# Grouped-query attention on one core: every matmul as a 64-row tile of the array, q, k and v cast by DMA, q and k also transposed by it, and the order of work fixed in the program

## The chip, the cores and the metric

The kernel runs on one core of a Trainium2 chip. Its time is device time in microseconds (us), the median of several runs. The profile is one execution, and its span is about 1.8 us shorter than the time of the same run. In this text PE or TensorE is the matmul engine, ACT or ScalarE computes the exponentials, DVE or VectorE the normalization, POOL or GpSimd issues DMAs that cast, and SP or SyncE issues the others.

## The reference

```python
batch, n_q_heads, n_kv_heads, seq, head_dim = (8, 8, 2, 1024, 64)   # q, k, v in f32, times 0.1
# four query heads share a key/value head
scores = scale * np.matmul(q_group, k_group.transpose(0, 1, 3, 2))  # scale = 1/8
attn = np.exp(scores - scores_max)
attn = attn / (np.sum(attn, axis=-1, keepdims=True) + 1e-08)
output = np.matmul(attn, v_group)
```

Both kernels leave out the maximum, which is harmless with inputs this small, and get the denominator from a column of ones beside v. A **cell** is 128 keys by 512 queries of one head; there are 8 x 8 x 2 x 8 = 1024. Three cells share one exponential instruction.

## The kernel before

It loads q, k and v as f32, transposes q and k on TensorE, and lets a scheduler order everything by priority. One side of a head pair is selected by a k that is padded with zeros to 128 rows.

```python
    def transpose_group(stages, lo, name_pool):          # 64 of these
        tp = tpool.tile([128, NSC, 128], BF16, name="tpsum")
        for sc in range(NSC):
            nc.tensor.transpose(tp[:, sc, :], _hi16(stages[sc])[:, lo : lo + 2, :], ident)
        dst = name_pool.tile([128, NSC, 128], BF16, name="xT")
        nc.vector.tensor_copy(out=dst, in_=tp)
    ...
    def score_wave(gw, qT, kT):
        sps = spool.tile([128, CPERW, QBS], FP32, name="spsum")       # two buffers
        with tc.high_priority(offset=1 << 20):                        # scores go first
            for slot, gc in enumerate(cells):                         # three cells
                nc.tensor.matmul(sps[:, slot, :], lhsT=kT[b][g][side][:, c, :],   # 128 rows
                                 rhs=qT[(b, pair)][...], start=True, stop=True)
        nc.scalar.activation(out=pt[:, 0:n, :], in_=sps[:, 0:n, :], func=AF.Exp, scale=scale)
    ...
    def output_block(b, pair, side, qb, pts, vt):        # 128 of these, 32 matmuls each
        ops = opool.tile([128, NQS, D + 1], FP32, name="opsum")       # one buffer
        for qs in range(NQS):
            for c in range(NKC):
                nc.tensor.matmul(ops[:, qs, :], lhsT=..., rhs=_hi16(vt[b][g][:, c, :]),
                                 start=(c == 0), stop=(c == NKC - 1))
        nc.vector.reciprocal(out=rec, in_=ops[:, :, D])
        nc.vector.tensor_tensor(out=ost, in0=ops[:, :, 0:D], in1=rec..., op=ALU.mult)
```

The softmax here doesn't subtract the row's maximum and nothing guards it: scores larger than these inputs give would overflow.

## Time and profile before

| | before |
|---|---|
| time, median of 4 runs measured beside the changed kernel | 479.99 us (479.82 to 480.41) |
| exponentials | 342, ends 1.343 us apart |
| start of the first exponential | 13.8 us |
| time lost between exponentials | 3.2 us |
| from the end of the last exponential to the end | 4.5 us |

The last three rows are read from the trace. I take the end of every exponential, subtract it from the next end, and call what exceeds 1.343 us lost. The sum must close: 13.8 + 3.2 + 4.5 = 21.5, and 480.1 - 21.5 = 458.6 us is the exponentials' own work.

The profiled execution, with its span of 480.1 us, was some 2 us slower than the median run.

### The profile page before, as it was taken

Reading aid. Unit: us, or ns where it says so; the run is one execution under the profiler, and the core shown is the slowest. Engines: PE = TensorE matmul, PEld = TensorE weight load, DVE = VectorE, ACT = ScalarE, POOL = GpSimd, SP = SyncE. Lnnn points to the kernel's source line nnn. Section 1 sums busy time; section 2 is a strip of 40 time slices with the busy share of each in tenths; the row PEclk is TensorE's granted clock in tenths of the full one; section 3 lists DMA queues with packets and bytes.
Section 4 is the critical chain, followed back from the end, with each engine's and each line's share of the span. In section 5 each row is a group of like instructions: output and inputs, shape, how many; then the busy total and the mean of one; then the engine's idle time right before and its main releaser. Section 6 shows DMA issues by size and latency. Waiting matters only on the chain.

```text
span 480.1 us, 13304 instructions
## 1 busy us (share of the span) xinstructions
PE 443.3 (92%) x5632; PEld 282.6 (59%) x5632; DVE 129.3 (27%) x400; ACT 460.2 (96%) x343; POOL 141.1 (29%) x198
## 2 busy tenths in 40 slices
PE   2999999999999999999999999999999998988895
PEld 1566666666666666666565656656565555555553
DVE  3332233232242323222241312313222111111112
ACT  1699999999999999999999999999999999999996
POOL 9993056128047111830138010111100111101011
PEclk9999999999999999999999999999999999999999
DMA  7997356138157122842148121211212111111111
GB/s 177 218 227 182 79 142 169 45 90 219 35 125 198 47 55 58 197 109 58 35 115 206 34 56 46 67 34 35 56 45 58 40 39 35 46 34 34 46 34 45
DMA packets 109883, 42.82 MB, mean 89 GB/s; under 512 B 105728, under 2 KB 105728, under 8 KB 109824
## 3 DMA queue, kind: packets, MB, share of 16 engines
q1 hardware_dynamic: 102656, 25.18, 24.8%
q0 software_dynamic: 7168, 16.79, 11.1%
q8 instruction: 44, 0.72, 0.6%
q14 instruction: 15, 0.12, 0.1%
HBM read 25.17 MB, written 16.78 MB: 87 GB/s over the span
## 4 chain that ended last, share of the span: by engine, by line
ACT 72%; PE 21%; issue 3%; POOL 1%; DMA 1%; DVE 1%; POOLq 0%
ACT pt L191 72%; PE spsum L183 13%; PE opsum L204 6%; PE tpsum L107 2%; POOL qstage L87 1%; DMA qstage<-in_q_dram 1%; DVE ost L216 0%; DVE xT L111 0%; DVE rec L214 0%; POOL ident masks.py:199 0%; POOL ident masks.py:197 0%; POOLq masks.py:199 0%; POOLq L277 0%
## 5 line engine op out<-in xcount | busy, mean ns | idle before, releaser
L191 ACT ACTIVATE pt<-spsum 128x1536 bf16<-128x1536 f32 x342 | 458.9, 1706 | 14.6 <-PE spsum L183 14.6
L183 PE MATMUL spsum<-xT 128*128 128x512 bf16 x1024 | 278.2, 380 | 23.5 <-ACT pt L191 19.0
L204 PEld LDWEIGHTS <-pt 128*128 128x128 bf16 x4096 | 174.0, 98 | 75.9 <-DVE ost L216 16.9
L204 PE MATMUL opsum<-vstage,pt 128*128 128x65 bf16 x4096 | 191.1, 195 | 1.1 <-DVE ost L216 1.0
L183 PEld LDWEIGHTS <-xT 128*128 128x128 bf16 x1024 | 98.5, 97 | 94.2 <-issue 35.8
L222 POOL DMA_DIRECT2D out_dram<-ost x64 | 48.3, 755 | 316.1 <-DVE ost L216 283.6
L214 DVE RECIPROCAL rec<-opsum 128x4 f32<-128x4 f32 x128 | 23.4, 183 | 309.2 <-PE opsum L204 300.4
L87 POOL DMA_DIRECT2D qstage<-in_q_dram x128 | 92.2, 723 | 18.4 <-PE tpsum L107 12.8
L216 DVE TENSOR_TENSOR ost<-opsum,rec 128x256 f32<-128x256 f32 x128 | 53.8, 421 | 3.7 <-DVE rec L214 0.2
L111 DVE COPY xT<-tpsum 128x1024 bf16<-128x1024 bf16 x64 | 43.6, 681 | 32.9 <-PE tpsum L107 20.7
L107 PE MATMUL tpsum<-ident,kstage 128*128 128x128 bf16 x256 | 28.5, 226 | 5.4 <-DMA kstage<-in_k_dram 5.3
L107 PE MATMUL tpsum<-ident,qstage 128*128 128x128 bf16 x256 | 27.4, 225 | 3.3 <-DVE xT L111 1.6
L107 PEld LDWEIGHTS <-kstage 128*128 128x128 bf16 x256 | 18.9, 101 | 14.0 <-issue 5.7
L107 PEld LDWEIGHTS <-qstage 128*128 128x128 bf16 x256 | 18.6, 101 | 9.8 <-issue 2.8
L77 DVE MEMSET kstage<- 128x192 f32 x64 | 13.5, 218 | 2.3 <-PE tpsum L107 0.9
L191 ACT ACT_TABLE_LOAD x1 | 1.3, 1283 | 0.7 <-PEq L277 0.7
L96 DVE MEMSET vstage<- 128x8 f32 x16 | 0.9, 65 | 0.0
masks.py:199 POOL TENSOR_SCALAR_AFFINE_SELECT ident<-ident 128x128 bf16<-128x128 bf16 x1 | 0.3, 307 | 0.1
masks.py:197 POOL MEMSET ident<- 128x128 bf16 x1 | 0.2, 205 | 0.3 <-POOLq L277 0.3
L277 POOL MEMSET const-float32-0.0<- 128x1 f32 x1 | 0.1, 99 | 0.2 <-issue 0.2
L277 POOL MEMSET const-bfloat16-1.0<- 128x1 bf16 x1 | 0.1, 102 | 0.0
L277 POOL MEMSET const-uint8-127<- 128x1 uint8 x1 | 0.1, 102 | 0.0
(1 smaller groups left out, 0.1 us busy)
## 6 DMA issues: line engine op xcount, KB each, us to landing
qstage<-in_q_dram POOLq DMA_DIRECT2D x128, 64.0 KB, 3.7
qstage<-in_q_dram SPq DMA_DIRECT2D x128, 64.0 KB, 3.4
out_dram<-ost SPq DMA_DIRECT2D x64, 128.0 KB, 1.9
out_dram<-ost POOLq DMA_DIRECT2D x64, 128.0 KB, 2.3
kstage<-in_k_dram SPq DMA_DIRECT2D x64, 64.0 KB, 2.7
vstage<-in_v_dram SPq DMA_DIRECT2D x16, 256.0 KB, 3.1
```

Of the source, the lines that this page charges most:

```text
L77: nc.vector.memset(ks[:, 0::2, :], 0.0)
L87: eng.dma_start(out=qstage[sc][:, 2 * j : 2 * j + 2, :], in_=q[b, 2 * j : 2 * j + 2].rearrange("h (sc p) d -> sc p h d", p=128)[sc],)
L96: nc.vector.memset(vs[:, :, D], 1.0)
L107: nc.tensor.transpose(tp[:, sc, :], _hi16(stages[sc])[:, lo : lo + 2, :], ident)
L111: nc.vector.tensor_copy(out=dst, in_=tp)
L183: nc.tensor.matmul(sps[:, slot, :], lhsT=kT[b][g][side][:, c, :], rhs=qT[(b, pair)][:, qb * NQS : (qb + 1) * NQS, :], start=True, stop=True,)
L191: nc.scalar.activation(out=pt[:, 0:n, :], in_=sps[:, 0:n, :], func=AF.Exp, scale=scale)
L204: nc.tensor.matmul(ops[:, qs, :], lhsT=pts[gc // CPERW][:, gc % CPERW, qs * 128 : (qs + 1) * 128], rhs=_hi16(vt[b][g][:, c, :]), start=(c ...
L214: nc.vector.reciprocal(out=rec, in_=ops[:, :, D])
L216: nc.vector.tensor_tensor(out=ost, in0=ops[:, :, 0:D], in1=rec.unsqueeze(2).to_broadcast([128, NQS, D]), op=ALU.mult,)
L222: (nc.gpsimd if (qb + side) % 2 else nc.sync).dma_start(out=out[b, h].rearrange("(qs p) d -> p qs d", p=128)[:, qb * NQS : (qb + 1) * NQS, :],
L277: nc = _bacc.Bacc("TRN2", target_bir_lowering=False, num_devices=1)
```

## The change

Its intent is to take work from TensorE. Two 64-row matmuls on the two halves of the array are meant to run side by side. The transposes leave TensorE for the DMA engines. The scheduler is switched off: the program's order is the order of every engine. The core of the diff, with cuts:

```diff
-            eng.dma_start(out=qstage[sc][...], in_=q[b, 2 * j : 2 * j + 2]...)   # f32, 64 KB each
-            nc.tensor.transpose(tp[:, sc, :], ..., ident)
-        nc.vector.tensor_copy(out=dst, in_=tp)
+        nc.gpsimd.dma_start(out=kscr..., in_=k[b]...)          # casts f32 to bf16, into DRAM
+        nc.sync.dma_start_transpose(out=kt, in_=kscr)
+        for j in range(NPAIR):                                 # four of q: five transposes in a row
+            nc.gpsimd.dma_start(out=qscr..., in_=q[b, j::NPAIR]...)
+            nc.sync.dma_start_transpose(out=qt, in_=qscr)
 ...
-                    lhsT=kT[b][g][side][:, c, :],
+                lhsT=kT[b][side * D : (side + 1) * D, c * 128 : (c + 1) * 128],
 ...
+        for c in (2 * part, 2 * part + 1):
+            for qs in range(NQS):
+                for rows in range(2):
+                    side = rows ^ half                         # the halves swap heads mid-unit
+                    lo = rows * 64
+                    mm = nc.tensor.matmul(
+                        ops[:, side, qs * (D + 1) : (qs + 1) * (D + 1)],
+                        lhsT=pcell[(u * NKC + c, side)][lo : lo + 64, qs * 128 : (qs + 1) * 128],
+                        rhs=vt[(b, side)][lo : lo + 64, c, :], ...)
+                    if half == 1 and c == 0 and qs == 0:
+                        tc.add_manual_dep(mm.ins, turn[0].name, SYNC, reason="bank")
+        if step == NKC // 2 - 1:
+            turn[0] = nc.sync.nop().ins                        # the turn
+            tc.add_manual_dep(turn[0], last.ins.name, SYNC, reason="bank")
 ...
+    with tc.manual_schedule():
+        load_batch(0)
+        for i in range(NSTEP + LAG):                           # 512 steps, LAG = 10
+                if i % per_batch == 4 and i // per_batch + 1 < B:
+                    load_batch(i // per_batch + 1)
+                score_step(i)                                  # two score matmuls
+                output_step(i - LAG)                           # sixteen output halves
```

A **unit** is now two heads by 512 queries, 16 cells, 8 steps; there are 64. A **step** is two scores and sixteen output halves. The **turn** is the moment in the middle of a unit when the halves of the array swap accumulators; TensorE then waits for a no-op on SyncE.

## The prediction

> **What bounds the kernel now.** I read the page first (busy times, then the chain that ended last), then the waits, then the groups, and last the timeline of a few microseconds in the middle.
>
> ```profile
> span 480.1 us, 13304 instructions
> ...
> PE 443.3 (92%) x5632; PEld 282.6 (59%) x5632; DVE 129.3 (27%) x400; ACT 460.2 (96%) x343; POOL 141.1 (29%) x198
> ...
> ACT 72%; PE 21%; issue 3%; POOL 1%; DMA 1%; DVE 1%; POOLq 0%
> ...
> L191 ACT ACTIVATE pt<-spsum 128x1536 bf16<-128x1536 f32 x342 | 458.9, 1706 | 14.6 <-PE spsum L183 14.6
> L183 PE MATMUL spsum<-xT 128*128 128x512 bf16 x1024 | 278.2, 380 | 23.5 <-ACT pt L191 19.0
> L204 PE MATMUL opsum<-vstage,pt 128*128 128x65 bf16 x4096 | 191.1, 195 | 1.1 <-DVE ost L216 1.0
> ```
>
> Two engines look full, but only one of them sets the time. ScalarE is idle 14.6 us before exponentials, in three places, and the list of waits shows that most of that is one gap, the start:
>
> ```profile
> ACT pt L191 <- PE spsum L183: 14.6, 3, 11.8
> PEld L204 <- DVE ost L216: 16.9, 60, 0.9
> ```
>
> Outside those three places an exponential follows the one before without a gap. Three of them take 4.41 us from the first start to the last end in the timeline below, and the median one lasts 1.727 us (the view of that line), so they start (4.41 - 1.727) / 2 = 1.343 us apart. 342 x 1.343 = 459.3 us. The first starts at 13.82 and the end comes about 4.5 us after the last: 13.8 + 459.3 + 4.5 = 477.6, plus some 2.5 us of early gaps. **The kernel is its exponentials.**
>
> ```profile
> 200.67 4.41 ACT L191 ACTIVATE pt<-spsum 128x1536 bf16<-128x1536 f32 x3
> 202.01 0.46 PE L204 MATMUL opsum<-vstage,pt 128*128 128x65 bf16 x9
> ...
> 202.44 0.81 PE L183 MATMUL spsum<-xT 128*128 128x512 bf16 x3
> ```
>
> TensorE's 92% is not its work. A score matmul is counted 380 ns, but three in a row take 0.81 us, so they start (0.81 - 0.38) / 2 = 0.215 us apart. Nine output matmuls take 0.46 us, (0.46 - 0.195) / 8 = 33 ns apart, weight load included. Work per exponential: 3 x 0.215 + 12 x 0.033 = 1.04 us of 1.343. TensorE has 0.3 us to spare per exponential, and the scheduler puts the three score matmuls of a tile together, directly after the wait for ScalarE. So a faster TensorE by itself can give nothing here: the most that remains to be won is at the start and the end.
>
> **What the Trainium skill says.** "ScalarE: Activation LUTs", section "What ACT_TABLE_LOAD costs", gives an ACTIVATE with immediate scale 186 ns + 0.833 ns per element, of which 93 ns overlap back to back: 1.37 us for 1536. The trace has 1.343, so it agrees and the engine is at its rate. "TensorEngine Tiling (Array Packing)", "Key Properties", says that different tiles can load weights and multiply in parallel; no run here shows it yet. "TensorE: Matmul & The Clock Gate", "LDWEIGHTS", says that a load costs by its columns, not its rows: a 64-row load of 128 columns would be no cheaper than a 128-row one, and the change doubles their number. "DMA: Bandwidth & Descriptors", "SWDGE vs HWDGE vs iDMA", says that a cast must be issued from GpSimd and a transpose from SP or ScalarE. That is how the change splits them, and it puts the transposes on SyncE, where something else now has to pass.
>
> **The change part by part.**
>
> Exponentials: 1024 cells in tiles of three, 342 instructions of the same shape. Unchanged, 459.3 us. This is the floor.
>
> Scores: still 1024 matmuls of 512 columns, now in pairs on the two halves of the array. If pairs overlap, 512 x 0.215 = 110 us instead of 220.
>
> Output: 4096 matmuls of 128 rows become 8192 of 64 rows. If halves overlap perfectly a half costs 33 / 2 = 16.5 ns, if not at all 33. I take 20 ns, an estimate that leans to overlap: 24 x 0.020 = 0.48 us per exponential. With the scores (1.5 x 0.215 = 0.32) TensorE needs 0.80 of 1.343 us, so it has 0.54 to spare. At 33 ns it would need 1.11, which still fits on average. Also gone are 512 identity transposes and 64 copies of 0.68 us on VectorE, neither on the path.
>
> Order: the program order is now fixed. TensorE has 2 scores, 16 output halves, 2 scores, and so on, where a scheduler pulled the scores forward before. Each score tile therefore has one block of 16 halves inside. From release to full tile: 0.22 + 16 x 0.020 + 0.38 = 0.92 us, against 0.81 now. The first two exponentials of the run, which find the engine empty, take 2.79 us together (timeline at 13.82), so one that is not queued lasts 2.79 - 1.343 = 1.45 us, and the round trip is 1.45 + 0.05 + 0.92 + 0.1 = 2.52 us for two tiles, below 2 x 1.343 = 2.69. Steady state holds, with little spare.
>
> The end of a unit: numerator and denominator of both heads of a unit share one accumulator with one buffer. After its last matmul come 0.195 us of latency, the reciprocal (0.19), the multiply, now 512 elements (0.42 for 256 today, so about 0.69), and hand-overs of about 0.1: 1.2 us. Only two scores (0.22) stand between, then the next output matmul waits for VectorE and **all later scores wait behind it**. Now that wait is 16.9 us in 60 times, and the scores are not behind it. TensorE stands about 0.95 us per unit, its spare time takes some 0.6 of that, 0.33 reach ScalarE: 64 x 0.33 = 21 us.
>
> The turn: halfway through a unit the two halves swap banks, and TensorE waits for a no-op on SyncE. SyncE runs in order and also issues the transposes and the stores. A plain DMA takes it about 0.55 us now (8 in 4.04, 12 in 7.70); I take 0.9 for a transpose, a guess. Five of them come in one lump of 4.5 us per batch, just ahead of a turn; some 1.8 us of it are hidden by the four steps before the turn and the full score tile. 6 batches x 2.7 = 16 us.
>
> The start: k must be cast into DRAM, land, be transposed, land, then q the same: two transfers in series in place of one transfer, TensorE and a copy. First exponential at 16.5 instead of 13.8. The first turn stands on SyncE behind the transposes of batch 1 too, and these wait for the twelfth cast on GpSimd's queue. One DMA issue costs GpSimd 0.72 us today, landing 3.7 us later. With 2048 pieces each I expect the twelfth at about 30 us, when TensorE wants the turn at 16.5 + 9 x 1.343 = 28.6 less the lead, so about 23. 7 us lost.
>
> The tail: ten steps of output lag, 10 x 16 x 0.020 = 3.2 us, plus the last VectorE pair and the store. About 5.5 us after the last exponential instead of 4.5.
>
> Sum: 16.5 + 459.3 + 21 + 16 + 7 + 5.5 = 525.3 us. **I predict 525 us, 9% slower.**
>
> **Rivals.** (1) The loops swallow everything: the VectorE wait is hidden in the 0.54 us of spare time and its neighbour, SyncE issues a transpose in under 0.4 us. Then only start and tail remain: 16.5 + 459.3 + 5.5 + a few = 482 to 488, "same". For it: ScalarE has a full second tile as a reserve. Against: in-order scores behind a 1.2 us wait, 64 times. (2) TensorE becomes the bound because weight loads do not overlap: 33 ns per half makes the tile 0.22 + 0.53 + 0.38 = 1.13 us, the round trip 2.73 > 2.69, and with the VectorE waits no longer hidden (0.7 per unit, 45 us) plus the turns the time is 550 to 565. For it: today's 33 ns may be the load's own time, and loads double. Against: the matmul's own 65 columns account for most of 33 ns too. (3) SyncE: a transpose takes 2 us to issue. Then each batch loses 8 us instead of 2.7, and the time is about 555. (4) Faster: only by an earlier start and no stall; at best 459 + 10 + 4 = 473, not 2% either, so faster by over 2% needs something I do not see, such as shorter exponentials.
>
> **Range and chances.** Low 486: rival 1 with a late start. High 567: rival 2 or 3. All terms of the sum are losses, the gain is off the path, so slower by over 2% (above 489.5) gets 0.86, same 0.11, faster 0.03.
>
> **What would show each step.** Spacing of exponentials inside a unit stays 1.343 and their count 342: steady state right. In the waits, ScalarE waiting for scores rises from 14.6 to some 60 us. Output weight loads or matmuls waiting for the VectorE multiply: about 40 to 60 us in 63 times. A wait for SyncE's no-op of several us, once per batch, and one longer near 25 us: turn right. Nine or so halves in a row with starts near 20 ns: overlap right; near 33: rival 2. DMA-transpose issue time on SyncE: 0.9 us or not. The prediction is wrong if ScalarE still shows no gaps after the start (rival 1), or if its spacing inside a unit grows above 1.4 us (rival 2).

## More of the kernel before

The prediction shows the page's main lines. Two rows of the page by slices (40 equal parts of the span, a digit is tenths) complete them, the busy share of ScalarE and the granted clock of TensorE:

```profile
ACT  1699999999999999999999999999999999999996
...
PEclk9999999999999999999999999999999999999999
```

ScalarE is full from the third slice to the last but one, and the row shows no fall of the clock (the trace's clock records begin at 21.1 us).

## The result

The changed kernel takes 546.62 us (545.11 to 547.14, four runs), against 479.99 us. The ratio is 1.136, with a 95% interval from 1.133 to 1.140: slower. (A ratio is the mean time of one kernel's runs over the mean of the other's runs of the same rounds, so it is not quite the ratio of the medians quoted.) Executions over 1.5% slower than the fastest of the same kernel are left out of the means. The result is correct. The same lines of the page after:

```profile
span 545.4 us, 19767 instructions
...
PE 357.6 (66%) x9216; PEld 228.7 (42%) x9216; DVE 57.5 (11%) x128; ACT 466.6 (86%) x343; POOL 98.2 (18%) x76
...
ACT  0547999699978999699996999959997899999994
...
PEclk9988999699996999889996999869999699899999
...
ACT 45%; PE 21%; issue 13%; DVE 7%; SPq 7%; DMA 4%; POOL 3%; ACTq 0%; POOLq 0%
...
L148 PE MATMUL ops<-vs,pt 64*128 64x65 bf16 x8192 | 260.0, 197 | 61.9 <-SPq L162 36.1
```

TensorE's busy time did fall, from 443.3 to 357.6 us, and VectorE's from 129.3 to 57.5. None of that reached the end, because ScalarE was the bound. ScalarE's busy time is 6 us more, its share of the chain fell from 72% to 45%, and its row shows a hole about every five slices, each with a fall of the clock in it or next to it. The list of waits (who waits for whom, total us, times, longest):

```profile
ACT pt L105 <- PE sps L125: 70.6, 61, 17.4
...
PEld L148 <- SPq L162: 58.1, 45, 10.9
PEld L148 <- DVE ost L175: 54.1, 56, 1.1
PE ops L148 <- SPq L162: 36.1, 7, 10.4
PE ops L148 <- DVE ost L175: 22.8, 38, 1.0
```

Both waits that the prediction named are there. The no-op on SyncE (L162) holds output matmuls in seven places for 36.1 us; VectorE's multiply (L175) holds them 38 times for 22.8. One end of a unit and one batch's lump follow each other in this stretch of the timeline (start, duration, engine, line, operation, count; in brackets the idle time before it and who ended that):

```profile
89.93 0.21 DVE L173 RECIPROCAL rec<-ops 128x8 f32<-128x8 f32 x1 [6.22 <-PE ops L148]
...
90.17 0.69 DVE L175 TENSOR_TENSOR ost<-ops,rec 128x512 f32<-128x512 f32 x1
...
90.92 0.42 PE L148 MATMUL ops<-vs,pt 64*128 64x65 bf16 x16 [0.37 <-DVE ost L175]
...
91.65 4.13 ACT L105 ACTIVATE pt<-sps 128x1536 bf16<-128x1536 f32 x3 [0.20 <-PE sps L125]
...
91.94 1.20 SPq L72 DMA_TRANSPOSE kT<-kscr  x1
...
93.25 5.26 SPq L81 DMA_TRANSPOSE qT<-qscr  x4
...
94.50 0.37 PE L125 MATMUL sps<-qT,kT 64*128 64x512 bf16 x1 [0.51 <-ACT pt L105]
...
98.62 0.62 PE L148 MATMUL ops<-vs,pt 64*128 64x65 bf16 x16 [3.75 <-SPq L162]
...
99.46 0.65 PE L148 MATMUL ops<-vs,pt 64*128 64x65 bf16 x16
...
99.77 1.45 ACT L105 ACTIVATE pt<-sps 128x1536 bf16<-128x1536 f32 x1 [3.98 <-PE sps L125]
```

From 91.94 to 98.51 SyncE does nothing but issue five transposes, and the turn's no-op is behind them. TensorE is stopped for 3.75 us, ScalarE for 3.98. After the stop sixteen halves take 0.62 to 0.65 us instead of 0.42. The trace's clock records say why: the granted clock is one half from 96.9 to 107.2 us. "TensorE: Matmul & The Clock Gate", section "Part 1: The HAM clock gate", of the Trainium skill says "the default state is throttled, and activity releases the throttle"; stops of this length and half-clock stretches of about 10 us at all six lumps agree with it. A long stop is not needed, though: the clock also fell for 3.4 us at 342.7 and at 465.6 us, where no lump is. In the 3.41 us before, TensorE was busy for 1.89 and 1.98 us; in the kernel before, no such stretch from its first clock record to 475 us had less than 2.6. No threshold comes out of this: with the turn moved (next section), a stretch with 1.77 us busy at 51.1 us passed at full clock. That the lighter load on TensorE itself costs clock at times is suggested, but no run tests it alone.

The start is later too:

```profile
7.09 1.29 SPq L72 DMA_TRANSPOSE kT<-kscr  x1
...
15.68 0.10 PEld L125 LDWEIGHTS <-kT 64*128 64x128 bf16 x1 [15.68 <-DMA kT<-kscr]
18.36 1.46 PE L125 MATMUL sps<-qT,kT 64*128 64x512 bf16 x6 [18.36 <-DMA qT<-qscr]
...
19.41 1.45 ACT L105 ACTIVATE pt<-sps 128x1536 bf16<-128x1536 f32 x1 [17.39 <-PE sps L125]
```

The account of the span, term by term beside the prediction:

| term | predicted us | measured us |
|---|---|---|
| first exponential starts | 16.5 | 19.4 |
| the exponentials themselves | 459.3 | 458.4 |
| ends of units | 21 | 10.8 (35 gaps of about 0.31) |
| SyncE's lump, batches 2 to 7 | 16 | 27.7 (six gaps, 4.09 to 4.96) |
| half clock after those lumps | not in it | 7.8 |
| first turn | 7 | 11.0 |
| other gaps (1.9 of it at the two short falls of the clock) | not in it | 3.0 |
| after the last exponential | 5.5 | 7.3 |
| sum | 525.3 | 545.4 |

### The profile page after: what moved, and what is told of

It is laid out like the page before. It is cut to its first block, busy times and chain, and to the rows that moved or that the text cites. A ratio compares the mean times of both kernels' runs of the same rounds, so it can differ in the third digit from the quotient of the medians.

```text
span 545.4 us, 19767 instructions
## 1 busy us (share of the span) xinstructions
PE 357.6 (66%) x9216; PEld 228.7 (42%) x9216; DVE 57.5 (11%) x128; ACT 466.6 (86%) x343; POOL 98.2 (18%) x76
## 4 chain that ended last, share of the span: by engine, by line
ACT 45%; PE 21%; issue 13%; DVE 7%; SPq 7%; DMA 4%; POOL 3%; ACTq 0%; POOLq 0%
ACT pt L105 45%; PE ops L148 12%; PE sps L125 9%; SPq L81 6%; DVE ost L175 5%; DMA qscr<-in_q_dram 4%; POOL qscr L76 2%; DVE rec L173 2%; POOL kscr L67 1%; SPq L72 0%; POOL vs L86 0%; ACTq L105 0%; POOL vs L85 0%; SPq L162 0%; POOLq L215 0%
## 5 line engine op out<-in xcount | busy, mean ns | idle before, releaser
L105 ACT ACTIVATE pt<-sps 128x1536 bf16<-128x1536 f32 x342 | 465.3, 1472 | 70.8 <-PE sps L125 70.6
L125 PE MATMUL sps<-qT,kT 64*128 64x512 bf16 x1024 | 282.7, 410 | 121.4 <-ACT pt L105 99.8
L148 PEld LDWEIGHTS <-pt 64*128 64x128 bf16 x8192 | 217.0, 98 | 225.7 <-issue 83.8
L148 PE MATMUL ops<-vs,pt 64*128 64x65 bf16 x8192 | 260.0, 197 | 61.9 <-SPq L162 36.1
L125 PEld LDWEIGHTS <-kT 64*128 64x128 bf16 x1024 | 79.4, 99 | 86.4 <-issue 70.5
L76 POOL DMA_DIRECT2D qscr<-in_q_dram x32 | 72.0, 4055 | 3.8 <-DMA kscr<-in_k_dram 1.8
L173 DVE RECIPROCAL rec<-ops 128x8 f32<-128x8 f32 x64 | 13.3, 208 | 482.1 <-PE ops L148 482.1
L175 DVE TENSOR_TENSOR ost<-ops,rec 128x512 f32<-128x512 f32 x64 | 44.2, 691 | 2.2
L67 POOL DMA_DIRECT2D kscr<-in_k_dram x8 | 16.5, 2058 | 0.9 <-POOLq L215 0.9
L86 POOL DMA_DIRECT2D vs<-in_v_dram x16 | 14.4, 897 | 9.6 <-POOL vs L85 5.9
```

The costliest lines, as they stand in the source:

```text
L67: nc.gpsimd.dma_start(out=kscr.rearrange("s (g d) -> s g d", g=G), in_=k[b].rearrange("g s d -> s g d"),)
L76: nc.gpsimd.dma_start(out=qscr.rearrange("s (g d) -> s g d", g=G), in_=q[b, j::NPAIR].rearrange("g s d -> s g d"),)
L86: nc.gpsimd.dma_start(out=vs[:, :, 0:D], in_=v[b, g].rearrange("(c p) d -> p c d", p=128),)
L105: nc.scalar.activation(out=pt[:, 0 : len(cells), :], in_=state["tile"][:, 0 : len(cells), :], func=AF.Exp, scale=scale,)
L125: nc.tensor.matmul(state["tile"][:, len(state["cells"]), :], lhsT=kT[b][side * D : (side + 1) * D, c * 128 : (c + 1) * 128], rhs=qT[(b, j) ...
L148: mm = nc.tensor.matmul(ops[:, side, qs * (D + 1) : (qs + 1) * (D + 1)], lhsT=pcell[(u * NKC + c, side)][lo : lo + 64, qs * 128 : (qs + 1) ...
```

## The experiments

All ran for at least three rounds beside the kernel before, whose median was 480.0 to 480.3 us each time.

### The turn on another queue

```diff
-            turn[0] = nc.sync.nop().ins
+            turn[0] = nc.vector.nop().ins
```

> The changed kernel with one word altered: the no-op that hands the two accumulator banks over is issued on VectorE (idle 89% of the time) instead of SyncE. My theory: the six gaps of 5.4 to 6.3 us and the one of 12.3 us between exponentials exist because that no-op stands on SyncE behind five transposes of about 1.2 us. Then all seven shrink to 1.3 to 1.7 us and the time falls by 11 + 6 x 5.9 = 46 us to about 500 us; the 0.3 us gaps at the end of every second unit stay. Rival A: the gaps come from the DMA traffic of the next batch, or from the half-rate TensorE clock that is granted after them; then they stay and the time stays near 546. Rival B: any hand-over through another engine costs this; then the gaps stay too.

Measured: 505.16 us (504.4 to 506.07), ratio 1.052. One word in the program is worth 546.6 - 505.2 = 41.4 us. The waits show what left:

```profile
ACT pt L105 <- PE sps L125: 30.3, 47, 16.4
PEld L148 <- DVEq L162: 21.3, 44, 0.8
```

The longest wait for the no-op is now 0.8 us and no gap between exponentials exceeds 3 us. The time lost between them fell from 60.3 to 19.1 us, and the mean granted clock rose from 0.927 to 0.992. In the account above the lumps, the half clock after them and the first turn make 27.7 + 7.8 + 11.0 = 46.5 us; all of it is gone, and about 5 us come back as other gaps, most of them in the first 85 us (8.0 instead of 3.0).

### The lump spread out

Here the no-op stays on SyncE, and the next batch's five transposes are issued one per unit, each right after a turn.

```diff
-            qt = qT_pool.tile([128, S], BF16, name="qT")
-            nc.sync.dma_start_transpose(out=qt, in_=qscr)
+            scrs.append(qscr)                                  # likewise for k
 ...
+                if i % 8 == 6 and i % per_batch < 40 and i // per_batch + 1 < B:
+                    transpose_one(i // per_batch + 1, i % per_batch // 8)
```

> The no-op stays on SyncE, but the five transposes of the next batch are issued one per unit, each directly after a no-op, instead of in one lump ahead of one. My theory (a lump of 6.5 us on SyncE): nearly the same result as with the no-op moved, 498 to 508 us. Rival A (DMA traffic): the bytes are the same, so part of the gaps stays, spread over the units. Rival B (SyncE is slow as a hand-over in itself): time stays near 546.

Measured: 504.45 us (503.94 to 505.0), ratio 1.051, the same as with the turn moved. So neither SyncE as such nor the bytes of the transposes cost anything that these times show: five of them in one run ahead of a turn do. The two experiments reach the same time by two different edits, so the cause is shown.

### Three scores at a time

```diff
-                score_step(i)
+                if i % 3 < 2:
+                    score_cells(2 * i + i % 3, 2 * i + i % 3 + 3)   # a whole tile of three
```

> The changed kernel with the three score matmuls of a tile issued together, and blocks of 16 output halves only between tiles; nothing else altered. My theory for the 47 gaps of 0.31 us at unit ends: a score tile is split by an output block that waits for VectorE, so its last score comes too late. With whole tiles the score tile is complete before the block that waits; these 15 us go, and the 46 us of the SyncE gaps stay: about 530 us. Rival: the gaps come from the length of the VectorE work itself in a single accumulator, whatever the order; then the time stays at 546.

Measured: 535.49 us (534.91 to 536.09), ratio 1.115, 11 us less than the changed kernel. Gaps of about 0.3 us fell from 35 to 14. One unit end in three (21) still shows a gap: twelve of 0.28 us, and nine of 0.45 to 1.41 us that all touch a half-clock stretch, seven of them a stretch of 3.4 us apart from the lumps. The wait for VectorE seems to hurt where a score tile is half full when TensorE stops.

### The first load later

```diff
-                if i % per_batch == 4 and i // per_batch + 1 < B:
+                if i % per_batch == (20 if i < per_batch else 4) and i // per_batch + 1 < B:
```

> Only the first lump is moved: batch 1 is loaded at step 20 instead of step 4, so that its casts and transposes stand behind the first no-op on SyncE rather than ahead of it. My theory: the gap of 12.3 us near 29 us goes, and the lump then delays a later no-op by about 5 us like in the other batches, or more if its casts have not landed: 538 to 546 us. The first exponential at 19.4 us does not come earlier, since the casts of batch 1 are issued after those of batch 0 anyway. Rival (the first gap is due to v or q landing late): the gap stays.

Measured: 549.84 us (547.36 to 551.01), ratio 1.146. A miss: I expected a gain. The first gap moved with the lump from 33.5 to 39.5 us and grew from 11.0 to 13.8 us. The lump stalls the turn that comes next, whichever that is, and in the first batch it also waits for its casts; moving it does not remove it.

### The order of the halves

```diff
-            for qs in range(NQS):
-                for rows in range(2):
+            for rows in range(2):
+                for qs in range(NQS):
```

> The changed kernel with the 16 output halves of a block in another order: four of the lower rows, then four of the upper rows, where the change alternates lower and upper. Same work, same banks, same waits; only the neighbours in the queue no longer lie on different halves of the array. It measures what 'two at a time' is worth. In the changed kernel 16 alternating halves take 0.42 us with the last one's latency, 15 ns apart. My theory: overlap needs alternation, so 16 halves take 0.6 to 0.7 us here (25 to 33 ns apart), the unit ends lose more, and the time rises by 15 to 45 us to 560 to 590 us. Rival: the spacing of 15 ns comes from cheaper 64-row loads; then it stays at 15 ns and the time at 546.

Measured: 545.1 us (544.79 to 546.84), ratio 1.135, no change; another miss of my theory. In both traces the starts of the halves form two interleaved rows, each with some 29 ns between starts, hence 15 ns on average. Why four of the same half in a row do not break this up stays open.

### Both output halves on the same 64 rows

```diff
-                    lo = rows * 64
+                    lo = 0                     # wrong result on purpose
```

> The changed kernel with both output halves taken from the lower 64 rows (a wrong result on purpose, same instructions, same shapes, same banks). The run with the halves in another order left open why 16 halves start about 15 ns apart whatever their order. Theory A (the two halves of the array run side by side, each at its own pace of about 29 ns, and the queue reaches several instructions ahead): with one half of the array alone the spacing doubles to 29 to 33 ns, 16 halves take 0.62 to 0.70 us, and the time rises to 560 to 590 us. Theory B (a 64-row load and matmul is simply cheaper than a 128-row one): the spacing stays at 15 ns and the time at 546 us.

Measured: 772.67 us (771.63 to 772.84), ratio 1.607, far above both ranges. Its output is wrong, which doesn't matter for the time. TensorE became the bound, but every matmul of the run was also as slow as in the half-clock stretch above. The same edit was therefore run on top of the moved turn, without stops of 4 us:

```diff
-            turn[0] = nc.sync.nop().ins
+            turn[0] = nc.vector.nop().ins
 ...
-                    lo = rows * 64
+                    lo = 0                     # wrong result on purpose
```

> The changed kernel with the turn on VectorE (505.2 us) and, on top, both output halves on the lower 64 rows (a wrong result on purpose). Question: was the 772 us of the same edit behind SyncE's lump a matter of the clock after long stops, or of the halves standing one after the other? Theory A, the clock: without the lump's stops of 5 us the run starts at full clock, halves start about 30 ns apart instead of 15, TensorE needs 1.5 x (16 x 0.030 + 0.35) = 1.25 us per exponential of 1.343, and the time is 530 to 565 us. Theory B, the load: a TensorE that never rests falls to half clock by itself, halves start about 54 ns apart as before and the time is 700 to 760. Theory C, no overlap existed: 503 to 508.

Measured: 748.46 us (748.15 to 748.96), ratio 1.558. From its page and from 300 us on its timeline:

```profile
PE 88%; DVE 7%; DMA 2%; issue 1%; ACT 1%; POOL 0%; DVEq 0%; POOLq 0%
```

```profile
300.45 0.97 PE L148 MATMUL ops<-vs,pt 64*128 64x65 bf16 x14
...
301.23 0.29 PE L148 MATMUL ops<-vs,pt 64*128 64x65 bf16 x2
...
301.75 0.97 PE L148 MATMUL ops<-vs,pt 64*128 64x65 bf16 x14
```

A step takes 301.75 - 300.45 = 1.30 us, and halves start (0.97 - 0.24) / 13 = 56 ns apart, with 0.24 the mean duration of one output matmul in this run, used for both kernels. Compare like with like, the half-clock stretch of the changed kernel: there a step takes 99.46 - 98.62 = 0.84 us and halves start (0.65 - 0.24) / 15 = 27 ns apart. Factor two: **halves on different rows do run side by side, halves on the same rows do not.** That is the point of the 64-row tiles, and it holds.

The clock of these two runs is inferred, not read: their traces hold no clock record at all, and the page then shows no clock row. Scores last 0.607 us in the mean of the whole run, as they do (0.58 to 0.61) in the changed kernel ahead of its first clock record, at about 32 us. I take it that the clock never came up, although TensorE was busy 91% of the span. So theory B had the time right, but a fall of the clock was not seen. Why half an array's work should not release the throttle is not settled.

### Score tiles alone, in the kernel before

```diff
-                    lhsT=kT[b][g][side][:, c, :],
-                    rhs=qT[(b, pair)][:, qb * NQS : (qb + 1) * NQS, :],
+                    lhsT=kT[b][g][side][side * D : (side + 1) * D, c, :],
+                    rhs=qT[(b, pair)][side * D : (side + 1) * D, qb * NQS : (qb + 1) * NQS, :],
```

> The kernel before with only its score matmuls made 64-row tiles (the zero half of k is left out), everything else as it was, scheduler included. My theory: the time is the exponentials', so faster scores gain nothing, and if switching between 64-row and 128-row tiles drains the array the cost falls into TensorE's spare 0.3 us per exponential: 478 to 484 us, same. Rival (the drain is large or scores of one head cannot overlap and lose more): over 490 us.

Measured: 488.94 us, the median of three runs of 488.53, 488.94 and 493.66 (a fourth, slow, took 509.63); ratio 1.021, interval 1.016 to 1.026, which straddles the 2% that counts as slower: unclear. A miss of the expected 478 to 484 us all the same. TensorE now has the larger part of the chain:

```profile
PE 462.9 (95%) x5632; PEld 252.8 (52%) x5632; DVE 129.0 (27%) x400; ACT 464.2 (95%) x343; POOL 141.1 (29%) x198
...
PE 62%; ACT 28%; DVE 4%; issue 4%; POOL 1%; DMA 1%; POOLq 0%
```

The first output matmul starts 0.304 us after the last score here, 0.215 before; the first score starts 0.125 us after the last output matmul, where neighbours start 33 ns apart. "TensorEngine Tiling (Array Packing)", "Key Properties", says "Mode switching requires drain". The trace agrees, at about 0.09 us one way and 0.09 the other. This kernel pays it twice per score tile. Not all of its loss lies there: of the 6.8 us more that it loses between exponentials (10.0 instead of 3.2), about 3 lie ahead of 30 us, where its first clock record comes at 27.0 us instead of 21.1.

### Whole output matmuls in the fixed order

The complement: on top of the moved turn, the output goes back to 4096 matmuls of 128 rows, and no turn is needed.

```diff
-        for c in (2 * part, 2 * part + 1):
-            ...                                # sixteen halves
+        c = step
+        for side in range(G):
+            for qs in range(NQS):
+                nc.tensor.matmul(ops[:, side, ...], lhsT=pcell[(u * NKC + c, side)][:, ...],
+                                 rhs=vt[(b, side)][:, c, :], ...)     # eight whole ones
-            turn[0] = nc.vector.nop().ins
```

> The changed kernel with the turn on VectorE (505.2 us), its output in 4096 whole 128-row matmuls, one chunk per step, no turn; scores stay in 64-row tiles. Question: what do the 64-row halves of the output buy in this order? Theory A, nothing, they fill spare time: a step needs 8 x 0.033 + 0.22 for the two scores + 0.22 for the change of tile size both ways + some 0.1 = 0.80 us of the 0.895 that two thirds of an exponential last, the time is 498 to 508, perhaps lower than 505 as the turn is gone. Rival B: the two changes of tile size per step, which cost 0.1 us each way in the kernel before with score tiles, put TensorE on the path: 515 to 540 and spacing inside a unit above 1.343.

Measured: 525.01 us (520.89 to 527.91), ratio 1.092, some 20 us more than with halves (505.16; measured in other rounds). Three steps' starts:

```profile
200.13 0.42 PE L145 MATMUL ops<-vs,pt 128*128 128x65 bf16 x8
...
200.48 0.39 PE L125 MATMUL sps<-qT,kT 64*128 64x512 bf16 x2
...
200.80 0.42 PE L145 MATMUL ops<-vs,pt 128*128 128x65 bf16 x8
```

Eight whole matmuls take the 0.42 us that sixteen halves take, so the halves as such save nothing. But a step lasts 200.80 - 200.13 = 0.67 us. In the changed kernel the scores of two steps that wait for nothing start at 91.50 and 91.96 us, 0.45 apart, the least distance in the trace and a frequent one. The difference, 0.22 us, is the two changes of tile size. Rival B had the time right and its mechanism half right: the spacing inside a unit stayed at 1.343 us, but the gaps at unit ends grew from 0.31 to about 0.73 us, probably since a slower TensorE makes up less of VectorE's wait.

### Attempts at a better version

The first puts the remedies together. The diff is cut to its main edits:

```diff
-    LAG = NKC + 2
+    LAG = NKC
+        # batch 0: k and q0 in halves first, other casts only after their transposes
+                if i % 8 == TR and i % per_batch >= 24 and i // per_batch + 1 < B:
+                    transpose_one(i // per_batch + 1, i % per_batch // 8 - 3)   # one per unit
+                score_cells(...)                                # three at a time
+                if (i - LAG) % NKC == 0 and i % 3 == 0 and i < NSTEP:
+                    late.append(i - LAG)                        # a unit's first block after the next scores
```

> The changed kernel with all suspected causes taken away together: transposes one per unit behind the no-op, score tiles whole, an output block that would stand between two score tiles at a unit's end put after the second, two steps less lag, and batch 0 loaded in halves with the other casts held back until these have landed. My theory: the gaps are gone (below 3 us in all after the start), the first exponential comes at 11 to 15 us instead of 19.4, the tail is 6 to 7 us: 12 to 15 + 459 + 2 + 6.5 = 479 to 484 us, the same as the kernel before. Rival (some cost lies in 64-row tiles or in the DMA casts themselves): 490 us or more remain.

Measured: 496.43 us (495.05 to 497.64), ratio 1.032, a miss. The first exponential starts at 12.4 us instead of 19.4. The version both splits the first loads in halves and holds the other casts back, and no run separates the two: k's first transpose is issued at 5.03 us instead of 7.09, and its data are usable 3.8 us later instead of 8.6. The lost time between exponentials is still 16.5 us, 9.8 of it in gaps that touch a half-clock stretch, and the tail 8.5.

The second moves one cell in sixteen from ScalarE to VectorE, with the polynomial the kernel before carries unused:

```diff
+        if state["due"] and n == 3:
+            state["due"] = False
+            n = 2
+            dve_exp(state["tile"][:, 2, :], pt[:, 2, :])        # eight VectorE instructions
```

> The same as the run with all causes removed, but one score cell in sixteen goes to VectorE, which computes the exponential with eight instructions in the formula that the kernel before carries unused; lag again ten steps. It uses the time that the change frees on VectorE. ScalarE then has 960 cells instead of 1024 and saves about 64 x 0.43 = 27 us: 455 to 462 us, if VectorE's eight instructions (about 4 us, an estimate from 0.69 us for its 512-column multiply) fit between two unit ends. Rival: the unit end's reciprocal and multiply stand behind them on VectorE, the accumulator is freed late, and the gaps come back: 480 us or more.

Measured: 504.77 us (503.35 to 505.24), ratio 1.050, a clear miss. ScalarE's busy time did fall, to 441.5 us, but it then waited for VectorE's reading of the score tile that both share:

```profile
ACT pt L186 <- DVE vxu L151: 42.8, 28, 10.8
```

The third is the first with the turn on VectorE, more of the blocks at unit starts deferred, v loaded before the second q, and batch 1's casts held until batch 0's last transpose has landed:

```diff
-            turn[0] = nc.sync.nop().ins
+            turn[0] = nc.vector.nop().ins
-                if (i - LAG) % NKC == 0 and i % 3 == 0 and i < NSTEP:
+                if (i - LAG) % NKC == 0 and i % 3 != 1 and i < NSTEP:
+            tc.add_manual_dep(kc.ins, after.ins.name, SYNC, reason="first")
```

> The run with all causes removed, mended where its trace still showed gaps: the no-op on VectorE, every unit's first output block put behind the next score tile, v cast before q1, and batch 1's casts held until batch 0's last transpose has landed. The earlier one lost 8 us in the first 70 us, 0.28 us at each third unit end (6 us) and 8.5 us after the last exponential. Theory: the gaps go and the tail stays: 12.5 + 459 + 2 + 8.5 = 480 to 484 us, the same as the kernel before. Rival: what is left comes from DMA traffic or the granted clock, and 490 us or more remain.

Measured: 490.88 us (490.63 to 492.92), ratio 1.022, interval 1.020 to 1.025, again near 2%. A miss of the expected 480 to 484 us, and the best version of the changed kernel. Its waits and its end:

```profile
ACT pt L156 <- PE sps L176: 18.5, 12, 10.2
```

```profile
480.65 3.60 PE L199 MATMUL ops<-vs,pt 64*128 64x65 bf16 x128 [1.03 <-DVE ost L226]
```

The unit ends are gone as a loss (three gaps of that size are left). Of the 10.1 us lost between exponentials 7.3 lie in the first 85 us and 8.6 in the first 97, while the first batches are loaded; which transfer each waits for I did not separate. In 7.3 of the 10.1 us the gaps touch half-clock stretches of 3.4 to 6.8 us; whether a slow clock makes them or follows from them is open too. The tail is 8.3 us, because the whole last unit, 128 halves, is computed after ScalarE has ended, most of it at half clock (480.2 to 483.6 us). No version ran faster than the kernel before.

## Why the prediction was right or wrong

**Right: the bound and the direction.** ScalarE was the floor and stayed it: 342 exponentials, 1.343 us apart inside a unit, 458.4 us against the predicted 459.3. (The last of the 342 holds one cell instead of three, which the prediction did not count; that is most of the 0.9 us.) TensorE's saving of 86 busy us was off the path. The measured time lies inside the range, and all of the change is loss, as the sum said.

**Right: the halves overlap.** The prediction's step took 20 ns per half; measured is (0.42 - 0.19) / 15 = 15 ns. A weight load takes 98 ns in the mean for 64 rows as it did for 128, as the prediction assumed. The runs with both halves on the same rows show the overlap at half clock, 27 against 56 ns. Rival 2 falls, since loads of different halves do overlap. What the prediction did not see is why the 64-row output pays: it spares the change of tile size, 0.22 us per step.

**Mis-sized: the turn.** The mechanism was named exactly, a no-op behind five transposes once per batch, and the hidden part was sized well. The guess of 0.9 us per transpose failed. SyncE took 1.20 us for k's and 5.26 / 4 = 1.3 for each of q's, so the lump is 6.57 us instead of 4.5. The six gaps average 27.7 / 6 = 4.6, which leaves 6.57 - 4.6 = 2.0 hidden where the prediction had 1.8. The term is 27.7 us instead of 16.

**Missing: what a stop does to the clock.** Each lump stops TensorE for nearly 4 us, and half clock follows for some 10 us. Steps take 0.84 us instead of 0.45, no spare time is left, and a further 1.1 to 1.8 us are lost per lump, 7.8 in all. No term of the sum had this, nor the two short falls of the clock away from the lumps.

**Mis-sized: the first turn and the start.** The cost of a cast was taken from today's 0.72 us per issue; with 2048 pieces instead of 256 GpSimd needs 2.05 to 2.3 us. The prediction also counted the transfers of k and q alone. In the trace k's transpose is issued at 7.09 us and usable only at 15.68, while casts of q fill the queues; a transpose lands in 3.7 us otherwise. The landing times of the casts by issue (queue, operation, count, KB, us to landing):

```profile
qscr<-in_q_dram POOLq DMA_DIRECT2D x32, 256.0 KB, 12.6
kscr<-in_k_dram POOLq DMA_DIRECT2D x8, 256.0 KB, 6.2
```

Start 19.4 instead of 16.5, first turn 11.0 instead of 7. For the turn it was the landing more than the issue that failed: GpSimd was done with batch 1's casts of q by 24.4 us, but SyncE began the last of batch 1's transposes only at 39.3. That the crowd of casts is the cause of the late start fits the version that held them back, which starts at 12.4; as that one also split the first loads, it is not shown by itself.

**Overestimated: the ends of units.** The size of one was right, 0.33 predicted and 0.31 measured, and the multiply takes the predicted 0.69 us. The count failed: 35 gaps, not 64. The list of ends shows them in two of three units, apart from those that fall into a lump; three units are exactly 16 score tiles, and in the third the stop meets a point where a tile is complete. That last reason is argued from the pattern and from the run with three scores at a time, where one in three is left, not shown by itself.

**Mis-sized: the tail.** 7.3 us instead of 5.5. The term had ten steps at 20 ns and VectorE once. In the trace the last 128 halves wait 1.03 us for VectorE at a unit end that nothing covers any more, then take 2.41 us, and VectorE and the store follow.

**Errors of opposite sign.** The unit ends came out 10 us too high; lumps and clock 19 us, first turn 4, start 3, tail 2 and other gaps 3 too low, and the exponentials 1 too high. Together that is the 20 us between 525 and the profiled 545.

## What to carry to other kernels

Look up which queue carries a synchronizing no-op and what else that queue has to issue ahead of it: here one word (another engine's queue), or one transpose per unit instead of five in a row, recovered 41 of the 67 us. An operation moved off an engine that was not the bound paid nothing here, and the fixed order turned waits on that engine into waits of the one behind it. Read the granted clock too: it fell at stops of TensorE, and at times without a long one. If 64-row tiles are used at all, keep every neighbouring matmul in them, because each change of tile size cost about 0.1 us here.

## What the Trainium skill lacked or had wrong

- "DMA: Bandwidth & Descriptors" gives the issue of a DMA transpose in cycles for small tiles and for one case within SBUF, but no time for a large one out of DRAM. SyncE took 1.20 us for one and 5.26 us for four, each 256 KB.
- The same page, "Anatomy of one DMA — SWDGE (gpsimd) path", says of descriptor generation "You can emit a lot of descriptors before the incremental cost shows up". Here a DMA of 256 pieces took GpSimd 0.72 us, a cast of 1024 pieces 0.90 us and one of 2048 pieces 2.05 us.
- "TensorEngine Tiling (Array Packing)" says that a change of mode drains the engine but not for how long: about 0.09 us each way in the kernel before with score tiles, 0.22 us for both in the fixed order.
- "TensorE: Matmul & The Clock Gate" speaks of busy and idle windows. It does not say what happens when only half of the rows are used: with both output halves on the same 64 rows, matmuls ran at what looks like half clock for 747 us, at 91% busy. This is inferred from durations, since the trace has no clock record. Nor does it say how little work counts as idle: in the changed kernel the clock fell after stretches of 3.41 us in which TensorE was busy for 1.89 and 1.98 us, and with the turn moved it stayed up after one with 1.77.